# Two contraction steps on one token tile before the next: a two-layer attention encoder on one core

## The chip, the cores and the metric

The kernel runs on one core of a Trainium2 chip. Its engines are TensorE (matmul, PE in the profile, with PEld for its weight loads), VectorE (DVE), ScalarE (ACT), GpSimd (POOL) and SyncE (SP, which here only issues DMAs). Each runs its own queue of instructions in order, and they wait for each other through semaphores. The metric is the device time of one execution in microseconds (us). Three runs of the kernel before took 844.46, 844.71 and 844.77 us, median 844.71.

## The reference, cut to what matters

Two encoder layers on 512 tokens of width 1024, in float32. Each normalises its input, makes queries, keys, values and a gate by one input projection, attends, multiplies by the gate's SiLU, projects back and adds the residual. Layer A attends in three dilated windows (16 heads x 3 groups, so 9 blocks of 1024 projection columns and 1024 for the gate), layer B in a two-dimensional neighbourhood (3 blocks and the gate).

```python
def mixer_a(hn, w_in, w_out, q_gain, k_gain, t5_bias):
    proj = hn @ w_in
    qkv = proj[..., :n_qkv].reshape(b, s, N_DIL_GROUPS, 3, N_HEADS, HEAD_DIM)
    gate = proj[..., n_qkv:]
    ...
    y = y.reshape(b, s, BRANCH_WIDTH).astype(hn.dtype) * jax.nn.silu(gate)
    return y @ w_out

def mixer_b(hn, w_in, w_out, q_gain, k_gain, rpb):
    proj = hn @ w_in
    q, k, v, gate = jnp.split(proj, 4, axis=-1)
    ...
    y = y * jax.nn.silu(gate)
    return y @ w_out

def reference(x, norm_gain, a_w_in, a_w_out, ...):
    for i in range(DEPTH):
        hn = rms_norm(x, norm_gain[i])
        ...
        x = x + y.astype(x.dtype)
    return x
```

## The kernel before

**Products.** A float32 product is made of three matmuls of reduced-precision halves: each operand is split into a high part and a rest, and `mm3` adds high x high, high x low and low x high into one PSUM bank. One such triple takes one contraction step (128 of the 1024 rows) on one token tile (128 tokens). All matmuls come from line 324 of the helper `matmul`, and all ScalarE, VectorE and GpSimd operations from line 85, so the profile is read by tile names.

**Banks.** PSUM has four banks for the projections (`acc`, pool `ps_acc`) and four for everything else (`log` for scores, `tp` for transposes, `o` for attention outputs). A bank is used again only when another engine has read it out; that reading is the `evac` of a product.

**Weights.** They arrive by DMA in pieces of up to 128 x 1024 into `wraw` (8 slots). ScalarE casts a step's piece to the high part `wh` (6 buffers), and GpSimd or VectorE, in turn, subtracts to make the low part `wl` (5 buffers). The generator `wsteps` hands out the next step's pair; calling it also issues casts, subtractions and loads some steps ahead.

**Order of work.** `main` yields after every triple of a projection, `side` is the attention (scores, softmax, weighting, normalisation). `run` and `pump` interleave the two on TensorE by a counted clock: after each triple the side work that has come due is issued. `yield guard` inside a product makes the side work run up to a named point before the product goes on. `chore` hands one half of a waiting SiLU (`silu`, on VectorE) to the queue. TensorE's order is that of the code; a scheduler places the other engines' instructions.

**Layer A.** A head pair's queries and keys and values of the two wider groups are made by a scheme with seven smaller products over half the tokens (256, two tiles) and half the contraction (four steps, `KH`). `product` is one of these: two banks, four steps. For a pair `hc` from 1 on they come in this order: the half product whose result `keep` holds, the gate (`project_t`), a second half product on the same banks (`put11`), the values of one group (`project_t`), four products on mixed operands (`mix_h`, `mix_l`, evacuated by `put_v`, `put_u`, `put12`, `put22`), and a last half product (`put21`) that goes on accumulating in the two banks which `put22` has to read out first. `rawq` and the `kv` halves (`rawk`) are their destinations. The first pair uses `project`, as layer B does.

**Layer B.** For each of eight head pairs, `project` makes queries, keys and values (384 columns, four token tiles, four banks, eight steps), evacuated by ScalarE (`rawk`, `rawb` or `rawq` by the head's number, `<-acc,rs_n`); then `project_t` makes the gate the other way round (one bank, eight steps of 24 matmuls, 512 tokens wide), evacuated by VectorE into `gt`. The pool hands the banks out in turn, so the gate takes the bank that the projection's tile 0 had, and the fourth tile of the next projection takes the gate's.

Around them stand two output projections, which this change doesn't touch.

Of the kernel before, what the change touches and what calls it, by code (L numbers as in the profile page):

```python
# [22 lines left out]
P = 128  # L23
# [4 lines left out]
KT = 8  # L28
# [5 lines left out]
KH = KT // 2  # L34
# [12 lines left out]
def tile_hybrid_encoder(  # L47
# [263 lines left out]
    def steps():  # L311
        for h, l, n in splits():
            for c in range(0, h.shape[1], n):
                yield h[:, c : c + n], l[:, c : c + n]
# [5 lines left out]
    def matmul(o, l, r, share=1, **kw):  # L320

        cols = max(r.free_size() / 2.4, l.free_size() / 1.2)
        clock[0] += (cols if r.dtype == F32R else r.free_size() * 4 / 2.4 * l.free_size() / P) / share
        nc.tensor.matmul(o, l, r, **kw)  # L324
# [5 lines left out]
    def mm3(o, lh, ll, rh, rl, first, last, **kw):  # L330
        matmul(o, lh, rh, start=first, stop=False, **kw)
        matmul(o, lh, rl, start=False, stop=False, **kw)
        matmul(o, ll, rh, start=False, stop=last, **kw)
# [21 lines left out]
    def chore(now):  # L355

        if now and chores and next(chores[0], "end") == "end":
            chores.pop(0)

    def product(acc, stat, open_, evac, guard=None):  # L360


        if open_:
            acc += [ps_acc.tile([P, 512], F32, tag="acc", name="acc") for _ in range(2)]
        for k in range(KH):
            chore(1 <= k < KH - 1)
            if k == KH - 1:
                yield guard
            h, l = next(wsteps)
            for i in range(2):  # L370
                sh, sl = (t[:, P * i : P * i + P] for t in stat(k))
                mm3(acc[i], sh, sl, h, l, open_ and k == 0, k == KH - 1, skip_group_check=True)
                if k == KH - 1:
                    evac(i, acc[i])
                yield

    def project(stat_h, stat_l, n, evac, guard, need=None, after=None):

        acc = {i: ps_acc.tile([P, 512], F32, tag="acc", name="acc") for i in range(4)}
        for k in range(KT):  # L380
            chore(1 <= k < KT - 2)
            if need:
                yield need, min(k + 1, KT - 1)
            if k == KT - 1:
                yield guard
            h, l = next(wsteps)
            for i in range(4):
                mm3(acc[i][:, :n], stat_h(k, i), stat_l(k, i), h, l, k == 0, k == KT - 1)
                if k == KT - 1:
                    evac(i, acc[i])  # L390
                yield
            if after:
                yield "xn", k
                after(k)

    def project_t(acc):

# [89 lines left out]
    wsteps = steps()  # L487
    wsteps = chain([next(wsteps)], wsteps)
# [128 lines left out]
    def project_qk(n, ns, key, hc, guard, first=False, **kw):  # L617

        box = []

        def evac(i, acc):
            if not box:
                box.append(raw_q() if key == "rawq" else part(0) if key == "rawk" else raw_b(hc, n))
                box.append(sums())
                held[0] = held[0] or (key == "rawk" and hc == 0)
            raw, ss = box
            dst, src = raw[:, i, :], acc[:, :n]
            if first:
                act.copy(dst, src)
                return  # L630
            act.activation(dst, src, AF.Copy, scale=rs_n[:, i : i + 1])
            (squares_soon if key != "raw" else squares)(raw[:, i, : ns * 64], ss, i, ns, key != "raw")

        tile_of = lambda hn: lambda k, i: hn[:, k, P * i : P * (i + 1)]
        yield from project(tile_of(hn_h), tile_of(hn_l), n, evac, guard, **kw)
        raw, ss = box
        if first:
            st["first"] = raw, ss
            stamp["first",] = clock[0]
            return  # L640
        normed(raw, ss, ns, key, hc)
# [45 lines left out]
    def main_a(hc):  # L687
# [40 lines left out]
        def put21(i, acc):  # L728
            t = kv[:, 2 + i, :]
            vec.tensor_add(t, t, acc)  # L730
            squares_soon(t[:, :256], box[0], 2 + i, 4)

        yield from product(a, hn(0, 0), True, keep, ("w", hc - 2))
        yield from gate_a(hc - 1)
        yield from product(a, hn(KH, 0), False, put11)
        if hc > 1:
            yield from v0_a(hc - 1, ("scored", hc - 1))
        for n, acc, first, put in ((0, c, True, put_v), (1, b, True, put_u), (3, c, False, put12), (2, b, False, put22)):
            yield "mix", n
            yield from product(acc, mixed(n), first, put, ("q", hc - 1) if n == 0 else None)  # L740
# [797 lines left out]
```

## Time and profile before

| what | value |
|---|---|
| median of three runs | 844.71 us |
| profiled execution, span | 844.7 us |
| mean granted TensorE clock | 0.999 |
| ScalarE busiest group: casts `wh<-wraw`, 360 | 209.5 us |
| GpSimd low parts `wl`, 153 of them, mean | 1.298 us |
| VectorE low parts `wl`, 207 of them, mean | 0.773 us |
| HBM read and written | 111.73 MB, 11.72 MB |

The busy share of an engine is an average over the whole span. TensorE overlaps neighbouring matmuls, and the length of one is modelled, so one matmul after another starts well before the one ahead is over: 0.39 us long at a distance of 0.23. What a matmul costs is therefore read from start to start. A note in square brackets behind a row of the timeline is the idle time ahead of it and what ended that; the view of waits adds these up by what was waited for.

### The profile page before, as it was taken

What the parts mean: (1) busy time and instruction counts of PE and PEld (TensorE: products, weight loads), DVE (VectorE), ACT (ScalarE), POOL (GpSimd) and SP (SyncE); (2) the same over time, 40 slices, a digit from 0 to 9 for tenths busy, and PEclk for the clock granted to TensorE, in tenths of its full rate; (3) what the DMA queues carried; (4) which work ended last, traced back from release to release, by engine and by line L of the source; (5) the groups of instructions that cost most, each with busy time, mean ns of one, the idle gap of its engine ahead of it and who ended that gap; (6) DMA issues with size and microseconds to landing.
All of it is one profiled execution on the core that took longest, in us unless ns stands there. A gap on an engine that the chain in (4) does not pass through costs nothing.

```text
span 844.7 us, 18126 instructions
## 1 busy us (share of the span) xinstructions
PE 829.5 (98%) x6611; PEld 686.0 (81%) x6611; DVE 631.8 (75%) x1653; ACT 508.2 (60%) x1066; POOL 291.7 (35%) x259
## 2 busy tenths in 40 slices
PE   9999999999999999999999999999999999999998
PEld 7877878878877878878877887789998898889786
DVE  7898997896995886896896876566668767776742
ACT  7656766846846846747747728554546664666440
POOL 5042343543533533533532514213123222322201
PEclk9999999999999999999999999999999999999999
DMA  9426766676676785785776554473265456644212
GB/s 342 141 57 170 190 155 151 141 172 195 133 172 201 158 194 167 159 205 132 162 177 167 119 186 144 150 237 111 93 192 161 132 146 180 173 135 115 85 51 100
DMA packets 56169, 131.97 MB, mean 156 GB/s; under 512 B 7184, under 2 KB 24528, under 8 KB 55952
## 3 DMA queue, kind: packets, MB, share of 16 engines
q1 hardware_dynamic: 49456, 108.39, 41.7%
q0 software_dynamic: 6048, 22.02, 15.3%
q8 instruction: 52, 0.85, 0.4%
q10 hardware_dynamic: 576, 0.41, 0.2%
q14 instruction: 37, 0.30, 0.1%
HBM read 111.73 MB, written 11.72 MB: 146 GB/s over the span
## 4 chain that ended last, share of the span: by engine, by line
PE 77%; ACT 8%; DVE 7%; DMA 4%; issue 2%; POOL 1%; SPq 0%; ACTq 0%; DVEq 0%; POOLq 0%
PE acc L324 64%; PE log L324 5%; PE o L324 4%; ACT p L85 4%; PE tp L328 3%; DMA wraw<-in_w 2%; ACT wh L85 1%; DVE wl L85 1%; DVE na L85 1%; DMA yr<-y_d 1%; ACT rawk L85 1%; DVE rawq L85 1%; DVE gt L85 1%; POOL sq L85 1%; DVE tr L85 1%
## 5 line engine op out<-in xcount | busy, mean ns | idle before, releaser
L85 POOL TENSOR_TENSOR wl<-wraw,wh 128x512 fp32r<-128x512 f32 (+1 forms) x153 | 198.5, 1298 | 434.8 <-PE acc L324 214.4
L85 ACT CAST wh<-wraw 128x512 fp32r<-128x512 f32 (+1 forms) x360 | 209.5, 593 | 194.7 <-PE acc L324 155.0
L85 DVE TENSOR_TENSOR wl<-wraw,wh 128x512 fp32r<-128x512 f32 (+1 forms) x207 | 159.3, 773 | 45.5 <-PE acc L324 33.3
L324 PE MATMUL acc<-wh,hn_h 128*128 128x384 f32 (+1 forms) x488 | 186.4, 382 | 2.7 <-DVE gt L85 1.5
L324 PE MATMUL acc<-wl,hn_h 128*128 128x384 f32 (+1 forms) x488 | 177.6, 364 | 1.7 <-DVE wl L85 1.7
L324 PE MATMUL acc<-wh,hn_l 128*128 128x384 f32 (+1 forms) x488 | 177.4, 364 | 0.0
L85 ACT ACTIVATE p<-p,mn 128x256 f32<-128x256 f32 (+2 forms) x248 | 137.7, 585 | 32.3 <-DVE mn L85 32.3
L324 PEld LDWEIGHTS acc<-wh,hn_h 128*128 128x128 f32 x488 | 92.1, 189 | 21.3 <-issue 6.8
L324 PEld LDWEIGHTS acc<-wl,hn_h 128*128 128x128 f32 x488 | 92.3, 189 | 10.0 <-DVE wl L85 2.6
L324 PEld LDWEIGHTS acc<-wh,hn_l 128*128 128x128 f32 x488 | 92.0, 189 | 9.8
L324 PE MATMUL acc<-wh,mix_h 128*128 128x512 f32 x224 | 89.1, 398 | 0.0
L324 PE MATMUL acc<-wl,mix_h 128*128 128x512 f32 x224 | 87.5, 390 | 0.0
L324 PE MATMUL acc<-wh,mix_l 128*128 128x512 f32 x224 | 87.4, 390 | 0.0
L324 PE MATMUL acc<-hn_h,wh 128*128 128x512 f32 x192 | 79.0, 412 | 0.3 <-ACT rawb L85 0.2
L324 PE MATMUL acc<-hn_h,wl 128*128 128x512 f32 x192 | 75.1, 391 | 0.0
L324 PE MATMUL acc<-hn_l,wh 128*128 128x512 f32 x192 | 75.0, 391 | 0.0
L85 DVE STREAM_TRANSPOSE pt<-p 128x512 f32<-128x512 f32 (+1 forms) x60 | 40.6, 687 | 23.5 <-ACT p L85 23.4
L85 DVE TENSOR_REDUCE ss<-sq 128x4 f32<-128x256 f32 (+1 forms) x96 | 46.1, 502 | 11.8 <-POOL sq L85 5.9
L324 PE MATMUL acc<-y_h,wh 128*128 128x512 f32 x128 | 51.9, 405 | 0.5 <-ACT gt L85 0.5
L324 PEld LDWEIGHTS acc<-wh,mix_h 128*128 128x128 f32 x224 | 42.0, 188 | 9.9 <-issue 1.6
L324 PE MATMUL acc<-y_h,wl 128*128 128x512 f32 x128 | 50.0, 391 | 0.0
L324 PE MATMUL acc<-y_l,wh 128*128 128x512 f32 x128 | 50.0, 390 | 0.0
(148 smaller groups left out, 1358.9 us busy)
## 6 DMA issues: line engine op xcount, KB each, us to landing
wraw<-in_w SPq DMA_DIRECT2D x95, 512.0 KB
wraw<-in_w POOLq DMA_DIRECT2D x42, 512.0 KB, 6.9
wraw<-in_w SPq DMA_DIRECT2D x38, 384.0 KB
pt<-pt SPq DMA_DIRECT2D x106, 64.0 KB
td<-tr SPq DMA_DIRECT2D x24, 224.0 KB
pt<-td SPq DMA_DIRECT2D x24, 224.0 KB
e<-l_d SPq DMA_DIRECT2D x32, 112.0 KB
e<-l_d SPq DMA_DIRECT2D x16, 128.0 KB
```

Source lines behind the costliest of these rows:

```text
L85: m = f(*args, **kw)
L324: nc.tensor.matmul(o, l, r, **kw)
L328: nc.tensor.transpose(o, i, ident)
```

## The change

`product` and `project` now take two steps at a time. They fetch two pairs of weights from `wsteps`, and each token tile gets both steps' triples, six matmuls on one bank, before the next tile. The work in all is the same: the same triples, in the same order for each bank. `project` keeps single steps where it was given `need` or `after`, which is the first head pair of layer A only. The guard now stands ahead of the last two steps instead of the last. The chores move: in `product` to the start and after tile 0 of the first two steps, in `project` to the start and after tile 1 of the pairs beginning at steps 2 and 4.

```diff
-        for k in range(KH):
-            chore(1 <= k < KH - 1)
-            if k == KH - 1:
+        for k in range(0, KH, 2):
+            chore(k == 0)
+            if k == KH - 2:
                 yield guard
-            h, l = next(wsteps)
+            ws = [next(wsteps) for _ in range(2)]
             for i in range(2):
-                sh, sl = (t[:, P * i : P * i + P] for t in stat(k))
-                mm3(acc[i], sh, sl, h, l, open_ and k == 0, k == KH - 1, skip_group_check=True)
-                if k == KH - 1:
-                    evac(i, acc[i])
-                yield
+                for n, (h, l) in enumerate(ws):
+                    sh, sl = (t[:, P * i : P * i + P] for t in stat(k + n))
+                    last = k + n == KH - 1
+                    mm3(acc[i], sh, sl, h, l, open_ and k + n == 0, last, skip_group_check=True)
+                    if last:
+                        evac(i, acc[i])
+                    yield
+                if i == 0:
+                    chore(k == 0)
 
     def project(stat_h, stat_l, n, evac, guard, need=None, after=None):
 
         acc = {i: ps_acc.tile([P, 512], F32, tag="acc", name="acc") for i in range(4)}
-        for k in range(KT):
-            chore(1 <= k < KT - 2)
+        both = 1 if need or after else 2
+        for k0 in range(0, KT, both):
+            ks = range(k0, k0 + both)
+            chore(1 <= k0 < KT - 2)
             if need:
-                yield need, min(k + 1, KT - 1)
-            if k == KT - 1:
+                yield need, min(k0 + 1, KT - 1)
+            if KT - 1 in ks:
                 yield guard
-            h, l = next(wsteps)
+            ws = [next(wsteps) for _ in ks]
             for i in range(4):
-                mm3(acc[i][:, :n], stat_h(k, i), stat_l(k, i), h, l, k == 0, k == KT - 1)
-                if k == KT - 1:
-                    evac(i, acc[i])
-                yield
+                for k, (h, l) in zip(ks, ws):
+                    mm3(acc[i][:, :n], stat_h(k, i), stat_l(k, i), h, l, k == 0, k == KT - 1)
+                    if k == KT - 1:
+                        evac(i, acc[i])
+                    yield
+                if i == 1 and both == 2:
+                    chore(1 <= k0 < KT - 2)
             if after:
-                yield "xn", k
-                after(k)
+                yield "xn", k0
+                after(k0)
```

How this moves the instructions at three places follows. The numbers behind a tile's name tell its buffers apart; `[waits ...]` names the engine whose semaphore an instruction waits for.

TensorE's order in layer B where a gate product (bank `acc_7995`) ends and the next head's projection (banks `acc_8067` to `acc_8070`, tiles 0 to 3) begins, before:

```order
L324 MATMUL acc_7995<-hn_h_92,wl_7830 128x512
L324 MATMUL acc_8067<-wh_7828,hn_h_92 128x384 [waits Activation_49]
L324 MATMUL acc_8067<-wl_7853,hn_h_92 128x384 [waits Pool_49]
L324 MATMUL acc_8067<-wh_7828,hn_l_93 128x384
L324 MATMUL acc_8068<-wh_7828,hn_h_92 128x384 [waits Activation_49]
L324 MATMUL acc_8068<-wl_7853,hn_h_92 128x384
L324 MATMUL acc_8068<-wh_7828,hn_l_93 128x384
L324 MATMUL acc_8069<-wh_7828,hn_h_92 128x384 [waits Activation_49]
L324 MATMUL acc_8069<-wl_7853,hn_h_92 128x384
L324 MATMUL acc_8069<-wh_7828,hn_l_93 128x384
L324 MATMUL acc_8070<-wh_7828,hn_h_92 128x384 [waits DVE_49]
```

And now, from tile 2 on (six rows each for tiles 0 and 1 stand ahead of these):

```order
L324 MATMUL acc_8069<-wh_7816,hn_h_92 128x384 [waits Activation_49]
L324 MATMUL acc_8069<-wl_7853,hn_h_92 128x384
L324 MATMUL acc_8069<-wh_7816,hn_l_93 128x384
L324 MATMUL acc_8069<-wh_7851,hn_h_92 128x384
L324 MATMUL acc_8069<-wl_7859,hn_h_92 128x384
L324 MATMUL acc_8069<-wh_7851,hn_l_93 128x384
L324 MATMUL acc_8070<-wh_7816,hn_h_92 128x384 [waits DVE_49]
```

The fourth bank's first matmul, which waits for VectorE, stood behind 9 matmuls of the new projection and now stands behind 18.

TensorE's order in layer A at the end of the product that `put22` empties (on the mixed operands, banks `acc_4333` and `acc_4334`) and the start of the one that goes on in the same banks (on `hn_h`), before:

```order
L324 MATMUL acc_4333<-wh_4431,mix_h_94 128x512 [waits Activation_49]
L324 MATMUL acc_4333<-wl_4449,mix_h_94 128x512 [waits Pool_49]
L324 MATMUL acc_4333<-wh_4431,mix_l_95 128x512
L324 MATMUL acc_4334<-wh_4431,mix_h_94 128x512
L324 MATMUL acc_4334<-wl_4449,mix_h_94 128x512
L324 MATMUL acc_4334<-wh_4431,mix_l_95 128x512
L324 MATMUL acc_4333<-wh_4447,hn_h_92 128x512 [waits DVE_49,Activation_49]
```

And now:

```order
L324 MATMUL acc_4333<-wh_4431,mix_h_94 128x512 [waits Activation_49]
L324 MATMUL acc_4333<-wl_4439,mix_h_94 128x512 [waits Pool_49]
L324 MATMUL acc_4333<-wh_4431,mix_l_95 128x512
L324 MATMUL acc_4334<-wh_4411,mix_h_94 128x512
L324 MATMUL acc_4334<-wl_4433,mix_h_94 128x512
L324 MATMUL acc_4334<-wh_4411,mix_l_95 128x512
L324 MATMUL acc_4334<-wh_4431,mix_h_94 128x512
L324 MATMUL acc_4334<-wl_4439,mix_h_94 128x512
L324 MATMUL acc_4334<-wh_4431,mix_l_95 128x512
L324 MATMUL acc_4333<-wh_4437,hn_h_92 128x512 [waits DVE_49,Activation_49]
```

Between the last matmul on the first bank and the next product's first on it stood three matmuls, now six; the last step's weights (`wh_4431`) are now asked for three matmuls earlier.

ScalarE's order in layer B at the evacuation of the first projection above (`rawk`; `p` and `mn` are the softmax of the head before), before:

```order
L85 ACTIVATE p_8211<-p_8211,mn_8212 128x256
L85 ACTIVATE p_8211<-p_8211,mn_8217 128x256
L85 ACTIVATE p_8222<-p_8222,mn_8223 128x256
L85 ACTIVATE p_8222<-p_8222,mn_8228 128x256
L85 CAST wh_8294<-wraw_8088 128x384
L85 ACTIVATE p_8261,mn_8262<-p_8261,mn_8262 128x256
L85 ACTIVATE rawk_160<-acc_8067,rs_n_97 128x384
L85 ACTIVATE p_8261,mn_8267<-p_8261,mn_8267 128x128
L85 ACTIVATE rawk_160<-acc_8068,rs_n_97 128x384
```

And now:

```order
L85 ACTIVATE p_8211<-p_8211,mn_8212 128x256
L85 ACTIVATE rawk_160<-acc_8067,rs_n_97 128x384
L85 ACTIVATE p_8211<-p_8211,mn_8217 128x256
L85 ACTIVATE p_8222<-p_8222,mn_8223 128x256
L85 ACTIVATE p_8222<-p_8222,mn_8228 128x256
L85 ACTIVATE rawk_160<-acc_8068,rs_n_97 128x384
L85 ACTIVATE p_8272,mn_8273<-p_8272,mn_8273 128x256
```

The two evacuations now stand ahead of softmax rows behind which they stood before.

## The prediction, made before the changed kernel was run

> **What bounds the kernel now.** I read the page first (busy shares), then the waits of the engine that is busiest, then the timeline of that engine around every place where two neighbouring big matmuls stand further apart than usual, and last the chain of waits around the few places where it waits long.
>
> The page's first lines and its chain:
>
> ```profile
> span 844.7 us, 18126 instructions
> PE 829.5 (98%) x6611; PEld 686.0 (81%) x6611; DVE 631.8 (75%) x1653; ACT 508.2 (60%) x1066; POOL 291.7 (35%) x259
> PE 77%; ACT 8%; DVE 7%; DMA 4%; issue 2%; POOL 1%; SPq 0%; ACTq 0%; DVEq 0%; POOLq 0%
> ```
>
> TensorE is busy 98% of the span and carries 77% of the chain. The change neither adds nor removes a matmul, so what it can win is only the time in which TensorE is held up, and what it can lose is new time of that kind. The profiled execution (844.7 us) is the median of the runs (844.71), so the sum below is made against 844.7.
>
> The waits of TensorE, with total, count and longest in us:
>
> ```profile
> PE log L324 <- ACT k L85: 2.0, 4, 0.8
> PE acc L324 <- DVE wl L85: 1.7, 2, 1.3
> PE acc L324 <- DVE gt L85: 1.5, 5, 0.4
> PE acc L324 <- DVE rawq L85: 1.2, 6, 0.2
> ```
>
> Two of these (`gt`, `rawq`) are waits for a PSUM bank that another engine is still emptying, and they come once per head. This view is too small for them: it counts a matmul as running until its modelled end, whereas what matters is the distance from start to start. The unit for that is the undisturbed pitch. One gate product puts 24 matmuls into one single bank, first and last:
>
> ```profile
> 102.93 0.39 PE L324 MATMUL acc<-hn_h,wh 128*128 128x512 f32 x1
> 108.15 0.39 PE L324 MATMUL acc<-hn_h,wl 128*128 128x512 f32 x1
> ```
>
> 5.22 us over 23 distances is 0.227 us for a matmul of 512 columns, all on the same bank. For 384 columns the pitch is 0.173 us (585.25 to 585.42 below). One step on one token tile is three matmuls: 0.68 us at 512 columns, 0.52 us at 384.
>
> **The change part by part.** It turns "one step for every tile, then the next step" into "two steps for one tile, then the same two for the next tile". So each bank gets six matmuls in a row. Staying on one bank costs nothing by the 24 matmuls above, so the reordering as such is priced at zero, and TensorE itself is its cover. [...]
>
> What changes is when a bank is first needed and when it is finished, at three kinds of border.
>
> *Border 1, gate product to the next head's projection, layer B.* The fourth tile's bank is the one that the gate product used, and VectorE empties it (`gt`):
>
> ```profile
> 646.45 0.34 PE L324 MATMUL acc<-wh,hn_l 128*128 128x384 f32 x1
> 647.16 0.45 PE L324 MATMUL acc<-wh,hn_h 128*128 128x384 f32 x1 [0.37 <-DVE gt L85]
> 647.45 0.34 PE L324 MATMUL acc<-wl,hn_h 128*128 128x384 f32 x1
> 646.42 0.68 DVE L85 TENSOR_TENSOR gt<-acc,rs_half 128x512 f32<-128x512 f32 x1
> ```
>
> The step 646.45 to 647.16 is 0.71 instead of 0.173, and the one behind it 0.29 instead of 0.173: 0.54 + 0.12 = 0.66 us, of which the view calls 0.37 a wait, so 0.29 comes on top of each listed wait. All five heads: 1.5 + 5 x 0.29 = 2.95 us. With the change the fourth tile is first touched after 18 matmuls instead of 9, that is 9 x 0.173 = 1.56 us later: at 646.45 + 0.17 + 1.56 = 648.18, while `gt` is done at 646.42 + 0.68 = 647.10. Slack 1.08 us; the whole 2.95 goes.
>
> *Border 2, a projection of layer B to its gate product.* The gate product's first bank is that of tile 0, which ScalarE empties:
>
> ```profile
> 585.25 0.33 PE L324 MATMUL acc<-wh,hn_l 128*128 128x384 f32 x1
> 585.42 0.39 PE L324 MATMUL acc<-hn_h,wh 128*128 128x512 f32 x1
> ...
> 611.22 0.56 ACT L85 ACTIVATE rawk<-acc,rs_n 128x384 f32<-128x384 f32 x1
> 611.47 0.34 PE L324 MATMUL acc<-wh,hn_l 128*128 128x384 f32 x1
> 611.83 0.50 PE L324 MATMUL acc<-hn_h,wh 128*128 128x512 f32 x1
> 612.16 0.39 PE L324 MATMUL acc<-hn_l,wh 128*128 128x512 f32 x1
> ...
> 749.68 0.34 PE L324 MATMUL acc<-wh,hn_l 128*128 128x384 f32 x1
> 750.04 0.50 PE L324 MATMUL acc<-hn_h,wh 128*128 128x512 f32 x1
> ```
>
> The first head's border (585) has no gap. Six later ones, 611 the first and 749 the last, have 0.36 - 0.173 = 0.19 and then 0.33 - 0.227 = 0.10: 6 x 0.29 = 1.75 us. The evacuation ends at 611.78 and the gate starts at 611.83, so this is again the bank. Tile 0 took its last matmul 9 x 0.173 = 1.56 us before 611.47; with the change it takes it 18 x 0.173 = 3.1 us before, and in ScalarE's new order the evacuation stands five rows earlier. ScalarE's idle share (40%) leaves room for that. I take the whole 1.75; if ScalarE still comes late, nothing of it.
>
> *Border 3, layer A, second mixed product to the fourth.* The next product accumulates nothing new into a bank until `rawq` has read it:
>
> ```profile
> 171.33 0.39 PE L324 MATMUL acc<-wh,mix_l 128*128 128x512 f32 x1
> 171.91 0.47 PE L324 MATMUL acc<-wh,hn_h 128*128 128x512 f32 x1 [0.19 <-DVE rawq L85]
> 172.22 0.40 PE L324 MATMUL acc<-wl,hn_h 128*128 128x512 f32 x1
> 171.08 1.37 DVE L85 TENSOR_TENSOR rawq<-rawq,acc 128x512 f32<-128x512 f32 x2 [1.10 <-PE acc L324]
> ```
>
> 0.58 - 0.227 = 0.35 and 0.31 - 0.227 = 0.08: 0.43, of which 0.19 is listed; six heads: 1.2 + 6 x 0.24 = 2.64 us. Tile 0's last matmul now starts three pitches before 171.33 (170.65), and its bank is free 1.26 us later (171.91). With the change it starts six pitches before the product's last, so 7 x 0.227 = 1.59 us before the next product's first. Slack 0.33 us, which is thin; VectorE waited 1.10 us for this tile, so nothing was queued ahead of it there. I take the whole 2.6; between 0 and 2.6 for the range.
>
> Gains together: 2.95 + 1.75 + 2.64 = 7.3 us, all three by the same reason.
>
> *What it costs: weights.* The second step of a pair is read three matmuls after the first, so 0.68 us earlier in layer A's half products (two tiles) and 1.56 us earlier in layer B's projections (four tiles); the first step's buffers are held as much longer. Layer B has room: this one was ready at 731.89 and used at 738.84, 6.95 us later.
>
> ```profile
> 731.34 0.55 DVE L85 TENSOR_TENSOR wl<-wraw,wh 128x384 fp32r<-128x384 f32 x1
> 738.84 0.33 PE L324 MATMUL acc<-wh,hn_h 128*128 128x384 f32 x1
> 71.64 0.40 PE L324 MATMUL acc<-wh,hn_h 128*128 128x512 f32 x1
> 73.34 0.49 PE L324 MATMUL acc<-wl,hn_h 128*128 128x512 f32 x1 [1.30 <-DVE wl L85]
> ```
>
> In the first mixed head of layer A, VectorE makes the low weights itself and is late once (71.64 to 73.34). There the earlier reading is lost in full: +0.7 us, bounds 0 and 0.7.
>
> *What it costs: loads.* A `wraw` slot comes free when the last low part made from it is written, and that write waits for its buffer, now read 0.68 us longer. Behind it hang a load, a cast, and in ScalarE's queue the `k` that the scores wait for (two rows of the chain of waits with start and length, then rows of the timeline):
>
> ```profile
> 248.84 0.94 POOL wl L85
> 249.77 9.49 DMA wraw<-in_w
> ...
> 259.36 0.62 ACT L85 CAST wh<-wraw 128x512 fp32r<-128x512 f32 x1 [6.17 <-DMA wraw<-in_w]
> 264.36 0.39 PE L324 MATMUL log<-k0h,q0h 64*128 64x256 f32 x1 [0.72 <-ACT k L85]
> 451.57 0.38 PE L324 MATMUL log<-k0h,q0h 64*128 64x256 f32 x1 [0.31 <-ACT k L85]
> 514.95 0.38 PE L324 MATMUL log<-k0h,q0h 64*128 64x256 f32 x1 [0.15 <-ACT k L85]
> 325.05 0.69 ACT L85 ACTIVATE k<-tp,gk 128x512 f32<-128x512 f32 x1
> 327.05 1.18 PE L324 MATMUL log<-k,q 64*32 64x128 f32 x64
> ```
>
> Three heads are stalled there already (264, 451, 515), so any delay d of the loads costs d in each. In a head without a stall, `k` is done at 325.74 and used at 327.05: 1.31 us of cover. With d up to one step on one tile, 0.68: between 0 and 3 x 0.68 = 2.0 us. I take two of the three heads in full, 1.4 us, since the chain runs without a break only at 249 to 264 and the other two waits are small.
>
> *The SiLU halves and two early weighings* move by a few matmuls. The former go on VectorE (25% idle), the latter six matmuls (1.4 us) ahead in two heads; nothing in the waits names them, so I price them at zero; without that cover one late weighing costs up to 1.4 us.
>
> Sum: 844.7 - 7.34 + 0.68 + 1.4 = **839.4 us**.
>
> **The rivals.**
>
> *Weights too late in layer A.* The tightest low part of a later head is done at 161.71 and used at 162.04:
>
> ```profile
> 160.42 1.29 POOL L85 TENSOR_TENSOR wl<-wraw,wh 128x512 fp32r<-128x512 f32 x1 [3.37 <-ACT wh L85]
> 162.04 0.39 PE L324 MATMUL acc<-wh,mix_h 128*128 128x512 f32 x1
> ```
>
> 0.33 us of margin against 0.68 asked for. If every one of the seven mixed heads pays 0.68 once, 4.8 us are lost: 839.4 + 4.8 = 844.2, no change. For it: that margin. Against it: in the whole run TensorE waits for low weights only twice, and the second step's cast also moves ahead in ScalarE's order, so the low part can start earlier.
>
> *Loads later by more, the slower side.* The place is the chain at 249 to 264. The slot's delay can be handed on: a load of 1,024 columns feeds two steps, and if each link (low part, load, cast) hands on 0.68 us, d is 2.04. Then three stalled heads pay 2.04 each and the five others 2.04 - 1.31 = 0.73 each: 9.8 us. 844.7 - 7.3 + 0.7 + 9.8 = 847.9. It cancels the gain from d = 1.65 us on (8d - 6.55 = 6.6), and is measurably slower from 1.86. For it: a cast that waits 6 us for its load in the row above. Against it: nothing in the edit repeats the 0.68 from link to link; a queue that is late by 0.68 is normally late by 0.68 at its end.
>
> *The gaps are not about order but about too few banks.* Then the fourth tile or the gate finds its bank taken all the same, and only the losses stay off or on: about 845. [...] Against it: 585.42 has the same banks and no gap, and the slacks of 1.08 and 0.33 us are worked out with the same number of banks.
>
> **How the numbers follow.** Forecast 0.75, weights 0.12, loads 0.09, banks 0.04. The forecast's own range is 836.0 (no cost at all, 837.4, and up to 1.4 of the 2.0 us of `k` waits gone as well) to 842.0 (border 3 stays, 2.6). The range that holds 8 in 10 reaches on to the weights' case: 836.0 to 844.3. A measurement of this kernel can tell some 0.2% (1.7 us) from no change, so below 843.0 is faster and above 846.4 slower: faster 0.75 (the forecast), same 0.16 (weights and banks), slower 0.09 (loads).
>
> **What would show it.** Right: the waits for `gt` and `rawq` are gone from TensorE's list; the first matmul on the fourth tile and the gate's first follow at 0.17 to 0.23 us; the wait near 73 is some 0.7 longer; the log waits for `k` grow by some 1.4 in total. Wrong: a wait for `wl` in most heads (weights), log waits of 6 us or more (loads), or the three gaps still there at the new places (banks).

## The result, and the profile after

The changed kernel took 850.54 us (median of 5 runs, 848.86 to 851.28) against 844.53 us (5 runs, 844.25 to 844.77): 1.0064 times as long, 95% interval 1.0053 to 1.0075. It is 6.0 us slower; the forecast was 5.3 us faster. All runs used below had a granted clock of 0.949 or more; one run of the changed kernel, at 0.754, took 1011.66 us and is left out.

The page of the kernel after, first lines and chain:

```profile
span 847.1 us, 18132 instructions
PE 826.6 (98%) x6611; PEld 686.3 (81%) x6611; DVE 631.0 (74%) x1653; ACT 507.8 (60%) x1066; POOL 294.2 (35%) x259
PE 82%; DVE 8%; ACT 4%; issue 2%; DMA 2%; SPq 0%; POOL 0%; DVEq 0%; ACTq 0%; POOLq 0%
```

The busy shares say nothing of it. The waits of TensorE in the kernel after (total, count, longest, in us) do:

```profile
PE acc L324 <- DVE wl L85: 4.8, 3, 3.0
PE tp L328 <- ACT vt L85: 2.2, 1, 2.2
PE log L324 <- ACT k L85: 2.0, 3, 0.7
PE o L324 <- issue: 0.9, 1, 0.9
PE tp L328 <- DVE gt L85: 0.8, 4, 0.2
PE acc L324 <- DVE rawq L85: 0.3, 1, 0.3
```

The wait for `vt` stood in this list before, but shorter:

```profile
PE tp L328 <- ACT vt L85: 0.8, 1, 0.8
```

`gt` as a wait for a bank (`acc`) is gone, and so are the six waits for `rawq`; the one left is at a new place, in the first mixed head (112.70). Those were the gaps that the forecast wanted to close. The waits for `wl` and `vt` are longer; an issue wait ahead of `o` and four short waits for `gt` ahead of a transpose are new; the `k` total is the same 2.0, but it sits elsewhere.

The three borders in the timeline of TensorE, kernel after (start, length, what):

```profile
178.48 0.39 PE L324 MATMUL acc<-wh,mix_l 128*128 128x512 f32 x1
178.77 0.47 PE L324 MATMUL acc<-wh,hn_h 128*128 128x512 f32 x1
...
618.26 0.33 PE L324 MATMUL acc<-wh,hn_l 128*128 128x384 f32 x1
618.43 0.39 PE L324 MATMUL acc<-hn_h,wh 128*128 128x512 f32 x1
...
654.10 0.33 PE L324 MATMUL acc<-wh,hn_l 128*128 128x384 f32 x1
654.27 0.33 PE L324 MATMUL acc<-wh,hn_h 128*128 128x384 f32 x1
```

Projection to gate (618) and the fourth tile (654) follow at the plain pitch, 0.17; the third border (178) is at 0.29 instead of 0.58.

One number of the comparison has to be put right first. The kernel before, profiled a second time (a run at 844.85 us), has this span:

```profile
span 842.9 us, 18126 instructions
```

In this and all other profiles with a time beside them, it lies 1.7 to 2.1 us above the span (838.85 and 837.1, 854.0 and 851.9). The profile of before that the prediction used has a span of 844.7 and was therefore, by this distance, of an execution some 1.8 us longer than the median; it is not the one to set against the profile after. The second profiles of both kernels are: 842.9 and 849.6.

Where the difference arises, read as the start of the n-th of the 3,096 matmuls into `acc` banks (counted from 0) in these two second profiles:

| n | before | after | after minus before | what stands between |
|---|---|---|---|---|
| 240 | 66.46 | 66.57 | 0.1 | start, first pair |
| 282 | 80.61 | 83.42 | 2.8 | wait for `wl` at 72, then half clock (0.50) |
| 300 | 86.95 | 90.81 | 3.9 | scores wait for `k` |
| 400 | 113.28 | 120.24 | 7.0 | `rawq`, `vt`, then half clock (0.51) |
| 432 | 125.56 | 134.87 | 9.3 | rest of the half clock (to 121.45), issue wait ahead of `o<-pt,v` (1.73) |
| 708 | 206.32 | 218.82 | 12.5 | `k` twice (1.0 each), issue wait (1.3) |
| 912 | 267.13 | 278.43 | 11.3 | an old stall for `k` is gone |
| 2100 | 596.16 | 607.37 | 11.2 | rest of layer A (the stall for `k` at 451 goes too, 1.1), out product |
| 3095 | 838.40 | 844.63 | 6.2 | layer B |

So layer B won 5.0 us, as forecast (4.7), and the first 200 us, in layer A, lost 12.5.

### The profile page after: what moved, and what is told of

The parts are those of the page before. It is cut to its first block, busy times and chain, and to the rows that moved or that the text cites. A ratio compares the mean times of both kernels' runs of the same rounds, so it can differ in the third digit from the quotient of the medians.

```text
span 847.1 us, 18132 instructions
## 1 busy us (share of the span) xinstructions
PE 826.6 (98%) x6611; PEld 686.3 (81%) x6611; DVE 631.0 (74%) x1653; ACT 507.8 (60%) x1066; POOL 294.2 (35%) x259
## 4 chain that ended last, share of the span: by engine, by line
PE 82%; DVE 8%; ACT 4%; issue 2%; DMA 2%; SPq 0%; POOL 0%; DVEq 0%; ACTq 0%; POOLq 0%
PE acc L324 69%; PE log L324 5%; PE tp L328 4%; PE o L324 3%; DVE rawq L85 2%; DVE wl L85 2%; DVE na L85 1%; DVE rs L85 1%; ACT wh L85 1%; DMA yr<-y_d 1%; ACT p L85 1%; DVE ss L85 1%; DVE rawk L85 1%; DMA pt<-in_xt 1%; ACT sq L85 0%
## 5 line engine op out<-in xcount | busy, mean ns | idle before, releaser
L85 POOL TENSOR_TENSOR wl<-wraw,wh 128x512 fp32r<-128x512 f32 (+1 forms) x153 | 194.1, 1269 | 401.1 <-PE acc L324 173.8
L85 DVE TENSOR_TENSOR wl<-wraw,wh 128x512 fp32r<-128x512 f32 (+1 forms) x207 | 165.0, 803 | 36.4 <-PE acc L324 21.3
```

What stands on the lines that cost most here:

```text
L85: m = f(*args, **kw)
```

## The experiments

All times are medians, with the ratio to the kernel before on the same chip.

**Which half loses.** Only `project` as changed, `product` as before (first run), and the other way round (second run).

```diff
 # first run: the kernel before with
-        for k in range(KT):
+        for k0 in range(0, KT, both):      # and the rest of the change to project
 # second run: the kernel before with
-        for k in range(KH):
+        for k in range(0, KH, 2):          # and the rest of the change to product
```

> Only `project` takes two steps per tile, `product` is as before. Theory 1 (all of the loss arises in layer A's `product`, because two weight casts are put into ScalarE's queue at once and stand ahead of what the scores need) and theory 2 (the loss comes from the guard that stands one step earlier in `product`) both expect the gain of layer B alone: the two repeating gaps there gave 4.9 us between the two traces, so 844.5 - 4.9 = 839.6 us (839 to 840.5). A theory that staying on one bank costs time of its own, or that layer B's weights come late, expects 844 or more.

> Only `product` takes two steps per tile, `project` is as before. If the parts add up, 850.5 + 4.9 = 855.4 us (854 to 857), with the waits for `gt` (1.5 us in five places) back and those for `rawq` gone but one. If the two parts hinder each other instead, less than 853.

Layer B alone: 839.63 us, ratio 0.9943 (0.9928 to 0.9959), in the expected range. Layer A's products alone: 853.42 us, 1.0100 (1.0084 to 1.0116), a little under the expected range. The loss is all in `product`; the two ratios multiply to 1.0042, which within their intervals is the 1.0064 of the whole change. Staying on one bank and layer B's earlier weights cost nothing that shows.

**The early fetch.** `product` keeps its pairs on TensorE but calls for the second step's weights only when tile 0 is about to use them.

```diff
-            ws = [next(wsteps) for _ in range(2)]
+            ws = []
             for i in range(2):
-                for n, (h, l) in enumerate(ws):
+                for n in range(2):
+                    if i == 0:
+                        ws.append(next(wsteps))
+                    h, l = ws[n]
```

> The changed kernel, but `product` fetches the second step's weights only when the first tile is about to use them, three matmuls later; TensorE's order is the same. Theory 1: one cast instead of two stands ahead of `k` in ScalarE's queue, so the three new waits of the scores for `k` (0.65 us each, at 84, 146 and 211, some 1.04 us of TensorE's time each) go, 3.1 us; the old stalls of later heads (2.2, 0.7 and 0.5 us in the trace of before) can come back, so the time is between 847 and 851. Theory 2 (guard): the three waits stay, 850.5.

843.11 us, ratio 0.9977 (0.9965 to 0.9989): 7 us less than the changed kernel, more than expected. Of the waits for `k` only one of 0.15 us, behind layer A's last head (517), is left; in this profile a wait of 1.37 us for `k0l` (511) stands beside it. ScalarE's queue shows why the others went. Kernel after, then this one:

```profile
142.97 0.62 ACT L85 CAST wh<-wraw 128x512 fp32r<-128x512 f32 x1
143.01 0.60 PE L328 MATMUL tp<-ident,rawk 128*128 128x128 f32 x4
145.04 0.62 ACT L85 CAST wh<-wraw 128x512 fp32r<-128x512 f32 x1 [1.46 <-PE acc L324]
145.57 0.68 ACT L85 ACTIVATE k<-tp,gk 128x512 f32<-128x512 f32 x1
146.30 0.39 PE L324 MATMUL log<-k0h,q0h 64*128 64x256 f32 x1 [0.65 <-ACT k L85]
```

```profile
139.40 0.62 ACT L85 CAST wh<-wraw 128x512 fp32r<-128x512 f32 x1
140.47 0.69 ACT L85 ACTIVATE k<-tp,gk 128x512 f32<-128x512 f32 x1 [0.45 <-PE tp L328]
141.87 0.62 ACT L85 CAST wh<-wraw 128x512 fp32r<-128x512 f32 x1 [0.70 <-PE acc L324]
```

In the kernel after, two casts stand ahead of `k`, and the second has to wait 1.46 us for TensorE to be done with a `wh` buffer; the transposes that `k` reads (`tp`) are done at 143.61, but `k` starts at 145.57, behind the casts, and the scores wait. With the later fetch, the cast that has to wait stands behind `k`.

The converse: the kernel before, with TensorE's order untouched, fetching two at once.

```diff
-            h, l = next(wsteps)
+            if k % 2 == 0:
+                ws = [next(wsteps) for _ in range(2)]
+            h, l = ws[k % 2]
```

> The kernel before with one change: `product` fetches two steps' weights at once, at every second step. TensorE's order stays as it was. Theory 1 (the early fetch is the cause): what the later fetch won back, 850.5 - 843.1 = 7.4 us, is lost here too: 844.9 + 7.4 = 852 us (850 to 853.5), with new waits of the scores for `k`. If the loss needs the matmuls in pairs: 845.

851.77 us, ratio 1.0083 (1.0070 to 1.0096): the size is as expected, the place is not. There is no new wait for `k`. The waits for `rawq` grew instead, from 1.2 us in six to 3.7 us in seven, and the wait for `wl` in the first mixed head from 1.30 to 2.28 us, with half clock behind it (mean granted clock of this execution 0.998). VectorE ahead of one of the waits for `rawq`, and the matmul that it holds up:

```profile
175.35 1.60 DVE L85 TENSOR_TENSOR wl<-wraw,wh 128x512 fp32r<-128x512 f32 x1
176.88 1.27 DVE L85 TENSOR_TENSOR rawq<-rawq,acc 128x512 f32<-128x512 f32 x2
177.70 0.47 PE L324 MATMUL acc<-wh,hn_h 128*128 128x512 f32 x1 [1.14 <-DVE rawq L85]
```

Here it is a low part that stands in VectorE's queue ahead of the evacuation for which TensorE waits. So theory 1 holds for the cause, the fetch of two steps at once, and falls as far as it named one victim: what stands behind the earlier casts and low parts in the queues of ScalarE and VectorE comes late, `k` in one order and `rawq` in the other. These rows are of single places; not every part of the 7 us was followed to its row.

**Guard and SiLU halves.** The guard alone later (first), then with the later fetch and with the SiLU halves at their old places (second).

```diff
-            if k == KH - 2:
-                yield guard
...
+                    if last and i == 0:
+                        yield guard
 # second run also, with the later fetch
-            chore(k == 0)
+            chore(k == 2)
```

> The changed kernel, but the guard in `product` stands directly ahead of the last step's triple on tile 0 instead of ahead of the last pair. Theory 2: the weighing `o<-pt,v` of the second head no longer stands directly behind `o<-pt,rawk`, and the 0.94 us of issue wait at 191 goes, and with it what the early side work cost around 110 to 122 (3.7 us): 846 to 848. Theory 1: the waits for `k` stay, and no more than 1.1 us is won: 849.4 to 850.5.

> The kernel of the later fetch, with the guard ahead of the last step on tile 0 and the SiLU halves at the places in the count of triples that they had before: only TensorE's order in pairs is left of the change to `product`. If guard and SiLU halves are what is left of the loss, 839.6 (layer B alone) - 2.6 (the waits for `rawq`) = 837 us (836.5 to 839). If the earlier reading of the second step's weights is, no better than the later fetch alone: 841.5 to 843.5.

The guard alone: 849.92 us, 1.0059 (1.0045 to 1.0074), some 0.6 us less than the changed kernel, within what theory 1 expected; theory 2 falls as the main cause. The issue wait was not in this profile, as theory 2 expected, but a wait for `gt` ahead of a transpose took its place (2.2 us in total, longest 1.4). The second: 845.80 us, 1.0014 (1.0005 to 1.0022), some 3 us worse than the later fetch with the change's own guard and halves (1.0014 against 0.9977), and outside both expectations. Putting these two back is no gain; which of the two does the harm was not tried.

**The first mixed head.** Most of what the later fetch leaves of the loss lies at 72 to 78 us, so here the first mixed head takes one step at a time again and the others take pairs with the later fetch.

```diff
+        paired[0] = hc > 1
...
+        return (product_pairs if paired[0] else product_steps)(*args)
```

> The kernel of the later fetch, but the first mixed head of layer A takes one step at a time as before. If what is left of the loss arises there (some 3.1 us between the traces of layer B alone and of the later fetch by 126 us, behind the longer wait for `wl` at 72 to 74 and the half clock that follows it), the time is 843.1 - 3.1 = 840.0 us (839 to 841), and TensorE stays at full clock around 75. If it arises in every head, 842 or more.

840.45 us, ratio 0.9949 (0.9937 to 0.9961), as expected. The wait for `wl` in question, in the kernel after:

```profile
70.98 0.40 PE L324 MATMUL acc<-wh,hn_h 128*128 128x512 f32 x1
74.33 0.50 PE L324 MATMUL acc<-wl,hn_h 128*128 128x512 f32 x1 [2.95 <-DVE wl L85]
```

It was 1.30 us before. In the later-fetch run it was 2.6, followed by a stretch at half clock; in this run it is 1.3 again with full clock behind it. The windows of two microseconds (busy time and count of PE, PEld, DVE, ACT, POOL, then the granted clock, DMA share, GB/s), later fetch first, this one second:

```profile
74.00:76.00 2.00, 2.00 (x7) 1.50 (x8) 2.00 (x4) 2.00 (x5) 0.00 (x0) 0.64 0.26 84
```

```profile
74.00:76.00 2.00, 2.00 (x12) 1.38 (x11) 2.00 (x4) 2.00 (x5) 0.00 (x0) 1.00 0.26 87
```

Seven instructions against twelve in the same time, with TensorE "busy" throughout in both.

**Border 3 for itself.** Layer B in pairs, and of layer A only the last two steps of the `put22` product (first); then also the product behind it, from the second mixed head on (second). Both fetch at use.

```diff
 # both, as written in the second: steps that start a pair are named to product
-            yield from product(acc, mixed(n), first, put, ("q", hc - 1) if n == 0 else None)
+            yield from product(acc, mixed(n), first, put, ("q", hc - 1) if n == 0 else None, pairs=(2,) if n == 2 else ())
 # second run only
-        yield from product(b, hn(KH, H), False, put21)
+        yield from product(b, hn(KH, H), False, put21, pairs=(0, 2) if hc > 1 else ())
```

> Layer B in pairs, and of layer A only the last two steps of the one product whose banks are read out while the next one waits (`put22`), with the second step's weights fetched at their use. The six waits for `rawq` go at no other cost: 839.6 - 2.6 = 837.0 us (836.3 to 838). If the reading of that product's last weights a triple earlier costs what it wins: 839.6.

> As the run with layer B and one product, but from the second mixed head on the product behind it (`put21`) takes two steps per tile too, so that its second bank is wanted three matmuls later; all of layer A's pairs fetch at their use. If the gap had only moved from the first bank to the second (0.32 us won and 0.29 us lost again per head in the trace of that run), the six gaps now go for good: 839.6 - 6 x 0.32 = 837.7 us (837 to 838.8). If another wait takes their place again: 839.6 or more.

840.22 us (0.9952, 0.9936 to 0.9968) and 839.59 us (0.9940, 0.9926 to 0.9954): neither is measurably better than layer B alone, and the 837 that was hoped for is missed. In the first, the gap only moved on by one bank:

```profile
299.58 0.39 PE L324 MATMUL acc<-wh,mix_l 128*128 128x512 f32 x1
299.80 0.39 PE L324 MATMUL acc<-wh,hn_h 128*128 128x512 f32 x1
300.03 0.39 PE L324 MATMUL acc<-wl,hn_h 128*128 128x512 f32 x1
300.26 0.39 PE L324 MATMUL acc<-wh,hn_l 128*128 128x512 f32 x1
300.75 0.50 PE L324 MATMUL acc<-wh,hn_h 128*128 128x512 f32 x1
301.08 0.40 PE L324 MATMUL acc<-wl,hn_h 128*128 128x512 f32 x1
300.00 0.69 DVE L85 TENSOR_TENSOR rawq<-rawq,acc 128x512 f32<-128x512 f32 x1 [0.67 <-PE acc L324]
```

The first bank follows at 0.22 now (299.58 to 299.80), but the second bank's evacuation runs to 300.69, and TensorE stands before it: 0.49 and 0.33 instead of 0.23, which gives back 0.36 of the 0.43. In the second run the wait is gone from the list in all six heads and some 0.4 us per head are won from 816 on to 1,680 matmuls; yet one wait for `gt` is new (1.1 us of TensorE's time, row below), the stall for `k` around 264 costs 0.5 us more than in the profile of layer B alone, and waits between 506 and 511 (`k0l`, `q0l`, `gt`) cost another 1.0:

```profile
190.79 0.66 PE L328 MATMUL tp<-ident,rawq 128*128 128x128 f32 x4 [0.95 <-DVE gt L85]
```

So a version that beats both kernels is layer B in pairs alone (839.63), and nothing tried in layer A added to it.

**The kernel before and the changed kernel once more.**

> The kernel before, once more, for a profile beside the others. In the other experiments the time of the profiled execution lies 1.75 us above its span (838.85 and 837.1, 854.0 and 851.9 are examples). If the profile of before that the prediction used was an ordinary execution, this one's span is 844.7 again and its time 846.4; if that profile was a slow execution, the span is 842.8 to 843.3 at a time of 844.5 to 845, with TensorE at full clock from the start.

> The changed kernel once more, for a time beside the runs on this chip and a second profile. The same order of instructions as before gives the same waits: 850.5 us (849 to 851.5), the wait for `wl` of 2.9 us at 71, that for `vt` of 2.2 us at 114, and TensorE at half clock for some 3.4 us behind one of them or both.

The first: 845.02 us against 844.39, ratio 1.0007 (0.9998 to 1.0016), span 842.9, which is the second case of the expectation. The clock at the start, however, is not what made the difference: the first profile, with matmuls 0.43 us apart up to 10.34 and 0.23 behind that, lost 1.4 us there and had it back by the 54th matmul, since `wl` was waited for instead. What is left in the end arose in a longer stall for `k` at 263 (0.9 us) and in waits for `k0l`, `q0l` and `gt` at 509 to 514 that the second profile does not have (1.3), less 0.4 won around 451. The second: 850.70 us (median of three, 850.07 to 851.36), 1.0066 (1.0045 to 1.0088), with the waits expected and half clock behind both long ones (0.50 from 74 to 76, 0.51 from 118 to 120).

## Why the prediction was wrong

**Borders 1 and 2 (2.95 and 1.75 us): right.** All gaps are gone in every head, at 0.17 and 0.23 from start to start, and layer B alone is 5.3 us faster.

**Border 3 (2.64 us): right in mechanism, not in yield.** The gap shrank from 0.58 to 0.29, some 0.3 us in each of six heads, 1.8 in all. It is given back on the way: in four of these heads a transpose now waits 0.20 us for `gt`, some 0.4 us of TensorE's time each.

**"Layer B has room" and "staying on one bank costs nothing": right,** by the run with layer B alone.

**Weights in the first mixed head (+0.7): mis-sized.** The wait grew by 1.65 us, not 0.68, since VectorE also reached that low part 1 us later in its own order (first row before, second row after):

```profile
72.60 0.68 DVE L85 TENSOR_TENSOR wl<-wraw,wh 128x512 fp32r<-128x512 f32 x1
```

```profile
73.59 0.68 DVE L85 TENSOR_TENSOR wl<-wraw,wh 128x512 fp32r<-128x512 f32 x1
```

And behind this stall TensorE was at half clock in the second profile of the changed kernel (0.50 from 74 to 76) and not in the first (1.00); that cost another 1.3 us (7.88 and 9.17 us from the end of the wait to matmul 282). Together up to 3.0.

**Loads (+1.4): wrong.** The three stalled heads were not stalled longer; the stalls at 263 and 451 went (1.3 and 1.1 us between the second profiles). What came instead are the three waits for `k` at 84, 146 and 211, for the other reason, and in heads that the sum had as covered by 1.31 us. That cover was misread as well: the matmul that waits is `log<-k0h,q0h`, which stands ahead of the one at 327.05 that reads `k`. In that head its second group starts at 326.58, so the cover is 0.84 us.

**The step that failed** is the pricing of the fetch. The prediction took two calls for weights as "the second step is asked for 0.68 us earlier", a matter of margins of the weights, and read the casts that moved ahead in ScalarE's order as help. It did see `k` behind a cast in ScalarE's queue, but only where a load makes that cast late; what the casts and low parts that are now issued earlier stand ahead of, it did not ask. In the rows above both engines took their work in the order of their queues; a cast or a low part that had been put ahead of `k` or `rawq` made these late (`k` started 1.96 us after its transposes were done, TensorE waited 1.14 us for `rawq`), and more so where it had to wait for a buffer that TensorE still read (1.46 us). For `vt` the same is likely, but its rows were not followed. That fetch is worth 7 us here, shown in both directions.

**What the miss of 11.1 us is made of** (850.5 against 839.4): 7.4 us go with the later fetch (843.1), another 2.7 with single steps in the first mixed head (840.5), and the 1.1 left has no run of its own; both the yield that border 3 did not bring and the costs that the sum had put in fall into it.

**SiLU halves and weighings (0): wrong in sign at one place.** The weighing that now comes three matmuls earlier or directly behind another run of small matmuls met an issue wait (at the end of this document there is more on it), here in the kernel after:

```profile
188.50 1.21 PE L324 MATMUL o<-pt,rawk 32*64 32x128 f32 x64
189.64 0.68 PE L324 MATMUL o<-pt,v 128*64 128x64 f32 x15
191.26 1.67 PE L324 MATMUL o<-pt,v 128*64 128x64 f32 x49 [0.94 <-issue]
```

**The baseline** (the profiled execution of 844.7 taken for the median of the runs) was wrong by some 1.8 us: a span is not a time, and this profile was not of a median run.

Of the rivals, the slower one (loads) had the right sign and the wrong chain, the weights' rival expected a wait for `wl` in every mixed head, and it came in the first alone (its margin was read too small: the row at 162.04 reads `wh`, and the first matmul on `wl` starts at 162.27, so 0.56 us, not 0.33); neither asked what is queued behind a cast. That the order alone could not help for want of banks is refuted by layer B, where the same banks gave 5.3 us.

## What to carry to other kernels

Where one change reorders the busiest engine and, by the way, changes when its inputs are called for, price the two apart: here the first was worth 5 us in layer B, the second cost 7 in layer A, and a fetch at the point of use won the 7 back, though not the 2.7 us that the earlier use itself cost in the first mixed head. In layer B the same fetch of two steps cost nothing that shows, so it has to be looked at place by place. For each instruction that moves ahead in an in-order queue, look at what it is moved past, what it may have to wait for there, and who waits for the ones behind it; a resource with spare busy time (ScalarE 60%) still delivered `k` late here, by those 1.96 us. And a gap closed at a bank was won here only where the next bank, and the next engine, were early enough (in the run with layer B and one product 0.36 of the 0.43 us was lost again at the second bank): follow the same stretch to the end of the head before it is booked.

## What had not been expected of the hardware

**Long stalls cost more than their length here.** The profiles hold eleven waits of TensorE of 2.2 to 3.0 us inside the kernel; in ten of them TensorE went to half clock for 3.41 us, from some time between 0.6 us before the end of the wait and 1.0 us after it. In the windows of the changed kernel, first profile, behind the wait for `vt` (116.54):

```profile
116.54 0.66 PE L328 MATMUL tp<-ident,vt 128*128 128x128 f32 x4 [2.18 <-ACT vt L85]
118.29 0.63 PE L324 MATMUL acc<-wl,hn_h 128*128 128x512 f32 x1
118.72 0.63 PE L324 MATMUL acc<-wh,hn_l 128*128 128x512 f32 x1
```

```profile
116.00:118.00 2.00, 1.46 (x8) 1.28 (x9) 1.80 (x7) 1.50 (x4) 0.92 (x1) 0.89 0.62 154
118.00:120.00 2.00, 2.00 (x7) 1.52 (x5) 1.86 (x6) 1.10 (x2) 0.37 (x1) 0.50 0.61 150
120.00:122.00 2.00, 2.00 (x67) 1.28 (x65) 2.00 (x4) 0.62 (x1) 0.43 (x1) 0.76 0.47 115
```

The distance is 0.43 instead of 0.227; a stretch of 3.41 us at half clock loses 1.7 us by this estimate, less where part of it falls into the wait (1.3 at 72). The second profile of the same kernel had it behind the wait for `wl` at 72 too (clock 0.92, 0.50, 0.73 in the windows from 72 to 78), the first profile did not, though the wait was the same 2.95 us:

```profile
74.00:76.00 2.00, 1.75 (x4) 1.46 (x5) 2.00 (x5) 2.00 (x5) 0.00 (x0) 0.50 0.27 93
```

Behind single waits of 1.2 to 1.7 us it was not seen (1.30 us in the first profile of before, clock 1.00 from 72 to 84). But the length of one wait did not decide it alone: in the run with layer B and one product, two waits of 1.0 and 0.7 us with few matmuls between them were followed by the half clock too (264.91 to 268.32):

```profile
263.50 0.38 PE L324 MATMUL log<-k0h,q0h 64*128 64x256 f32 x1 [1.02 <-ACT k L85]
264.60 0.39 PE L324 MATMUL log<-k0h,q0h 64*128 64x256 f32 x1 [0.71 <-ACT k L85]
```

```profile
266.00:268.00 2.00, 2.00 (x50) 1.52 (x35) 1.88 (x10) 0.00 (x0) 0.00 (x0) 0.50 0.05 12
```

In the second profile of the changed kernel the changes of the clock lie whole multiples of 3.41 us apart: they are at 5.40, 73.66, 77.08, 118.04 and 121.45, which is 20, 1, 12 and 1 times. Why the stretches have this length, and why the same wait of 2.95 us was followed by one in this profile and not in the first, no run shows.

**Issue waits at runs of small matmuls.** Ahead of `o<-pt,v` TensorE waited 0.9 to 1.7 us for nothing that the profile shows, in the kernel after (both profiles) and in three other runs (0.2 in a fourth), and not in the kernel before or in layer B alone. In the run with pairs from the second mixed head on:

```profile
184.87 1.62 PE L324 MATMUL o<-pt,v 128*64 128x64 f32 x48 [1.58 <-issue]
```

In the second profile of the changed kernel it came also where three large matmuls stood between the two runs (1.73 us at 129.97), so that they follow directly on each other is not the condition. All five profiles of kernels with the changed guard have the wait; the two with the guard later in `product` have none and 0.2 us, and those in which `product` keeps its old guard have none. So where the guard puts the weighing bears on it.

One more thing in the traces goes with it. In all five the wait in the second mixed head (184 to 194) ends at the same place, the 2,753rd or 2,754th of TensorE's recorded instructions, and 1.3 to 1.6 us before that end a DMA packet of 16,384 bytes on the queue marked `instruction` was over; the wait at 129.97 ended 0.6 us after such a packet. In the six profiles with the old guard the same place was reached 1.7 to 2.5 us after that packet, and in the run with the guard alone later 1.4 us after it, without a wait. No run varied this, and the cause of the wait stays open.
